# Small experts of a mixture-of-experts layer: chunks of 1024 channels, one gather and one scatter for all four

## The chip, the cores and the metric

The kernel runs on one core of a Trainium2 chip. The metric is the device time of one launch in microseconds (us), lower is better. Before the change the median of three runs is 2088.52 us (2086.04 to 2092.03).

## What is computed

Two blocks in a row on 256 tokens of 1024 channels, in float32. The second layer of the first block ends in a mixture of eight experts (`moe_swiglu`), and the second block first works on a context of 256 tokens of its own, which depends on nothing of the first block. Cut to what matters here:

```python
logits = xf @ w_router; top_vals, top_idx = top_k(logits, 2); gates = softmax(top_vals)
# each token goes to two of 8 experts, D_MODEL = 1024, D_FF_EXPERT = 3584
y = (silu(xb @ w1[e]) * (xb @ w3[e])) @ w2[e]          # xb: tokens of expert e
out = segment_sum(y * gate, token)                     # added back to 256 tokens
```

## The kernel before

The experts are put in order of how many tokens they have, and get room for 256, 128, 128, 128, 32, 32, 32, 32 tokens (`CAPS`). The last four are the small experts. Each has 42 MB of weights (w1, w3, w2 of 1024 x 3584 floats), as much as the biggest has, for 32 tokens. All weights of the kernel come as raw tiles of 1 MB (128 partitions x 2048 floats) over SP's queue. A big product splits a raw tile on ScalarE and VectorE into a high and a low part (`whi`, `wlo`) and takes three fp32r products; the small experts take the raw tile (`sraw`) as it is, in plain f32, which the program turns into two TensorE instructions per product.

A small expert's 32 tokens are the stationary operand and fill 32 of the array's 128 columns. So four products, for four different quarters of the channels, stand side by side in four column groups (`tile_position=(0, 32 * j)`) and write 32 partitions each of one PSUM bank. `smalls` is a generator of steps: `up` multiplies a chunk of 512 channels by w1 (column groups 0 and 1, 256 channels each) and w3 (groups 2 and 3), tile by tile, with half of a raw tile from each matrix and so two transfers of 512 KB; then Tanh and two VectorE operations make the gated product `eg` (64 partitions). `down` of the chunk before transposes `eg` (`ptg`, L1312), copies it on ScalarE to `gT` and multiplies it at once by two tiles of w2 (`sy`); the sums stay in `yacc`. Every small expert gathers its own tokens (`gather_x`: products `pg` of the hidden rows with a 0/1 matrix `oh`, and `gather_T`: `pgT`, `pgs`) and scatters its result (`scatter`: four masked copies `og` and eight products `pz<-yacc`).

The steps are dealt out between the units of big products. `drive` runs units of n raw tiles and holds up to `nhl` tiles' parts ahead; after each unit `balance` runs n x `rate` small steps. There are two such stages. In the first (`Mc`, the context stage here) the big units are the second block's context layers, `WITH_CTX` = 3 steps to a unit. In the second (`Mx`, the first expert's stage) they are `expert256(0)`, `WITH_EXPERT` = 2. Small steps that are left run alone afterwards (`for _ in smalls: pass`, the tail here), and then `experts128` takes the three middle experts (`h`, `y`). A small tile goes through a ring of four buffers (`sraw="b"`), in which a load can only be issued when TensorE has finished with the tile four places earlier; SP issues loads strictly in the order of the program. `fence` keeps the next big product on TensorE behind the last product of the small step. Beside units and small steps there are side generators (attention, mLSTM, gates), whose steps `tick` deals out once per unit. Product names: `gT`, `gk`, `go` context products, `hps` and `acc` the first expert's up and down products.

Of the kernel before, what the change touches and what calls it, by code (L numbers as in the profile page):

```python
# [36 lines left out]
WITH_CTX, WITH_EXPERT, ATTEND, MLSTM = 3, 2, (2.5, 3), 4  # L37
# [6 lines left out]
def _shape_consts():  # L44
# [6 lines left out]
    c["iota2"] = np.broadcast_to(np.arange(P) % 32, (P, P))  # L51
# [7 lines left out]
    c["quarter"] = (p // 32 == f[:, :4])  # L59
# [30 lines left out]
    moe = ("before", "iota", "iota2", "lt8", "eid", "caps", "quarter")  # L90
    names, packs = {}, []
    for part in (("ident",), early, late, moe):
# [80 lines left out]
class Kern:  # L173
    def __init__(self, ctx, tc, A, out):
# [9 lines left out]
        self.fence, self.in_small = None, False  # L184
# [32 lines left out]
    def drive(self, units):  # L217
        it, queue, held, nxt = iter(units), deque(), 0, None
        while True:
# [20 lines left out]
            if n:  # L240
                if self.later:
                    self.later.popleft()()
                self.tick()
# [12 lines left out]
    def tick(self):  # L256
        for s in list(self.sides):
            s.acc += s.rate
# [18 lines left out]
    def balance(self, big, small, rate):  # L277

        acc = 0.0
        for n in big:  # L280
            acc += n * rate
            while acc >= 1:
                self.in_small = True
                end = next(small, self) is self
                self.in_small = False
                if end:
                    break
                acc -= 1

# [56 lines left out]
    def mm(self, out, lhsT, rhs, start, stop, **kw):  # L346
        i = self.nc.tensor.matmul(out, lhsT, rhs, start=start, stop=stop, **kw)  # L347
# [47 lines left out]
    def gemm_out(self, loads, X, first, evict):  # L395
# [19 lines left out]
        def rest(w):  # L415
            first()
            for t in range(2):
                for n in range(2):
                    part(w[n], 0, n, t, False)
                    with self.lift():  # L420
                        evict(t, n, pts[t, n])
        for n in range(2):
            yield 1, prep(4, n), lambda w, n=n: half(w, n)
        yield 2, lambda: [prep(0, n)() for n in range(2)], rest
# [112 lines left out]
    def to_T_(self, z, X, tag, full):  # L537
        nc = self.nc
        for t in range(2):
            ts = slice(t * P, (t + 1) * P)  # L540
            for j in range(2):
                pt = self.bank(tag, "ptT")
                for kk in range(4):
                    k = 4 * j + kk
                    nc.tensor.transpose(pt[:, kk * P:(kk + 1) * P], z[:, t, k * P:(k + 1) * P], self.ident)
# [87 lines left out]
    def mixer(self, i, X, h, z1, e, S, ada):  # L633
# [58 lines left out]
        def p_T():  # L692
            pt = self.bank("a", "ptp")
            for k in range(2):
                for t in range(2):
                    nc.tensor.transpose(pt[:, k * 256 + t * P:k * 256 + (t + 1) * P], S.pin[:, t, k * P:(k + 1) * P], self.ident)
# [107 lines left out]
    def attn_side(self, i, S):  # L804
# [27 lines left out]
        for jp in range(2):  # L832
# [5 lines left out]
            for hh in range(2):  # L838
                pt = self.bank("c", "ptP")
                for h4 in range(4):  # L840
                    nc.tensor.transpose(pt[:, h4 * P:(h4 + 1) * P], s[:, hh * 4 + h4], self.ident)
# [183 lines left out]
    def moe(self):  # L1025
# [5 lines left out]
        with self.psum("M", a=4, s=2, b=2):  # L1031
# [4 lines left out]
            with (self.phase("Mc", 2, rows=1, wraw="xx", sraw="b"),  # L1036
                  tc.tile_pool(name="ctx", bufs=1) as self.hp):
                self.second_setup()
# [9 lines left out]
                self.balance(self.rest(), smalls, 1)  # L1048
# [32 lines left out]
    def first_rest(self, X):  # L1081
# [3 lines left out]
        def begin():  # L1085
# [5 lines left out]
            self.side(self.router(full, self.hp.tile([P, D], F32, name="route", tag="hs")), 3, 2000)  # L1091
# [22 lines left out]
    def gather_x(self, p, s0, cap):  # L1114

        nc, mp = self.nc, (self.smp if cap == 32 else self.mp)
        wide = max(cap, P)
        oh = mp.tile([P, 2, wide], F32, name="oh", bufs=2 if cap == 128 else 1)
        iota = self.C("iota2") if cap == 32 else self.C("iota")[:, s0:s0 + cap]
        for t in range(2):  # L1120
            nc.vector.tensor_scalar(oh[:, t], iota, self.place[:, t, p:p + 1], None, op0=ALU.is_equal)
        if cap == 32:
            x = mp.tile([P, 8, 32], F32, name="xs", bufs=2)
        else:
            x = [mp.tile([P, 8, cap], F32R, name=n, bufs=1 if cap == 256 else 2) for n in ("xeh", "xel")]
        per = min(8, 512 // cap)
        for j in range(8 // per):
            pt = self.bank("s" if cap == 32 else "a", "pg")
# [6 lines left out]
            if cap == 32:  # L1135
                nc.scalar.activation(x[:, sl], v, AF.Copy)
            else:
                self.split(x[0][:, sl], x[1][:, sl], v)
        return x, oh

    def gather_T(self, p, cap, oh):

        nc, mp = self.nc, (self.smp if cap == 32 else self.mp)
        nt = max(cap, P) // P
        ohT = mp.tile([P, nt, T], F32R if cap == 128 else F32, name="ohT", bufs=2 if cap == 128 else 1)
        gs = mp.tile([P, 2], F32, name="gs", bufs=4)
        pt = self.bank("s" if cap == 32 else "a", "pgT")
        for s in range(nt):
            for t in range(2):
                nc.tensor.transpose(pt[:, s * 256 + t * P:s * 256 + (t + 1) * P], oh[:, t, s * P:(s + 1) * P], self.ident)  # L1150
# [1034 lines left out]
```

## Time and profile before

| | before |
|---|---|
| median of 3 runs | 2088.52 us |
| profiled execution: its time, its span | 2086.75 us, 2085.0 us |
| TensorE busy, share of the span | 1957.8 us, 94% |
| VectorE, ScalarE busy | 66%, 49% |
| mean granted TensorE clock | 0.973 |
| DMA over the span | 541 MB, 260 GB/s |

Busy is the union of the instructions' spans on an engine, idle the rest. A row that gives a releaser says what ended the idle time just before an instruction. "PEclk" is the granted TensorE clock as a share of 2.4 GHz. Times are from the span's start. The small experts run from about 558 to 1296 us: the context stage from 558 to 893, the first expert's stage from 893 to 1253, the tail from 1253 to 1296.

### The profile page before, as it was taken

How to read it: one execution, taken by the hardware profiler on the slowest of the kernel's cores; microseconds unless marked ns; L12 is line 12 of the kernel's file. 1: busy time of each engine (PE TensorE's matmuls, PEld its weight loads, DVE VectorE, ACT ScalarE, POOL GpSimd, SP SyncE). 2: the span in 40 equal slices, each digit the busy share in tenths (PEclk: the TensorE clock that was granted, in tenths of full speed). 3: DMA queues.
4: the chain of work that ended last, by engine and by line, in shares of the span. 5: the costliest groups of instructions: out<-in, count | busy, mean ns of one | idle time of the engine just before them, and what ended most of it. 6: DMA issues, size and time to landing. Idle time of an engine off the chain costs nothing. (4 is left out here: it accounts for less than half of the span.)

```text
span 2085.0 us, 34522 instructions
## 1 busy us (share of the span) xinstructions
PE 1957.8 (94%) x13388; PEld 1557.5 (75%) x13388; DVE 1382.2 (66%) x2567; ACT 1013.3 (49%) x1696; POOL 85.3 (4%) x164
## 2 busy tenths in 40 slices
PE   6999999899998999899999997999999988998997
PEld 6768889687766676588878864787887858877876
DVE  8767445786657356645443433888888888887977
ACT  4534434344435333443333321767767745865774
POOL 1000000101000001000000000000000012011100
PEclk9999999899899999999999999999999999999999
DMA  8558785654797788998999999999999864334330
GB/s 288 171 195 298 243 287 195 218 165 135 258 325 263 261 283 302 323 349 326 385 383 377 335 343 356 388 355 331 346 341 335 320 209 129 100 110 122 102 101 31
DMA packets 302668, 541.13 MB, mean 260 GB/s; under 512 B 12688, under 2 KB 126112, under 8 KB 302240
## 3 DMA queue, kind: packets, MB, share of 16 engines
q1 hardware_dynamic: 301104, 534.73, 74.0%
q0 software_dynamic: 1104, 3.79, 0.6%
q8 instruction: 107, 1.75, 0.4%
q14 instruction: 65, 0.53, 0.1%
q10 hardware_dynamic: 288, 0.33, 0.0%
HBM read 533.33 MB, written 1.05 MB: 256 GB/s over the span
## 5 line engine op out<-in xcount | busy, mean ns | idle before, releaser
L335 DVE TENSOR_TENSOR wlo<-wraw,whi 128x1024 fp32r<-128x1024 f32 x572 | 677.7, 1226 | 178.8 <-ACT whi L334 175.3
L334 ACT ACTIVATE whi<-wraw 128x1024 fp32r<-128x1024 f32 x572 | 569.9, 1051 | 182.3 <-PE gT L347 44.1
L347 PE MATMUL gT<-xhi,whi 128*128 128x256 f32 x720 | 216.2, 302 | 17.1 <-ACT up L1641 9.7
L347 PE MATMUL gT<-xlo,whi 128*128 128x256 f32 x720 | 209.8, 292 | 1.4 <-DVE xlo L428 0.9
L347 PE MATMUL gT<-xhi,wlo 128*128 128x256 f32 x720 | 209.1, 293 | 0.0
L347 PEld LDWEIGHTS gT<-xhi,whi 128*128 128x128 f32 x720 | 142.5, 198 | 33.2 <-ACT up L1641 11.2
L347 PEld LDWEIGHTS gT<-xlo,whi 128*128 128x128 f32 x720 | 142.6, 198 | 3.2 <-DVE xlo L428 1.4
L347 PE MATMUL su<-sraw,xs 128*32 128x256 f32 x1792 | 138.1, 390 | 7.3 <-DMA sraw<-in_moe_w 6.6
L347 PEld LDWEIGHTS gT<-xhi,wlo 128*128 128x128 f32 x720 | 141.9, 198 | 3.0 <-issue 2.7
L347 PE MATMUL h<-wlo,xeh 128*128 128x512 f32 x336 | 133.1, 396 | 2.2 <-DVE wlo L335 2.2
L347 PE MATMUL h<-whi,xeh 128*128 128x512 f32 x336 | 132.2, 393 | 2.0 <-DVE z L1161 2.0
L347 PE MATMUL h<-whi,xel 128*128 128x512 f32 x336 | 131.4, 391 | 0.0
L347 PE MATMUL hps<-xeh,whi 128*128 128x256 f32 x448 | 128.4, 287 | 0.0
L347 PE MATMUL hps<-xel,whi 128*128 128x256 f32 x448 | 126.8, 283 | 0.0
L347 PE MATMUL hps<-xeh,wlo 128*128 128x256 f32 x448 | 126.6, 283 | 0.0
L893 DVE TENSOR_TENSOR gg<-gg,hps 128x256 f32<-128x256 f32 x50 | 20.9, 419 | 131.0 <-ACT gg L892 131.0
L347 PEld LDWEIGHTS su<-sraw,xs 128*32 128x32 f32 x1792 | 58.5, 111 | 59.1 <-DMA sraw<-in_moe_w 12.2
L347 PE MATMUL gk<-whi,xhi 128*128 128x512 f32 x240 | 99.6, 415 | 1.2 <-ACT whi L334 1.2
L347 PE MATMUL hps<-xhi,whi 128*128 128x256 f32 x352 | 100.2, 285 | 0.0
L347 PE MATMUL hps<-xlo,whi 128*128 128x256 f32 x352 | 99.6, 283 | 0.0
L347 PE MATMUL hps<-xhi,wlo 128*128 128x256 f32 x352 | 99.5, 283 | 0.0
L892 ACT ACTIVATE gg<-hps 128x256 f32<-128x256 f32 x50 | 19.0, 381 | 165.3 <-PE hps L347 163.5
(467 smaller groups left out, 4159.1 us busy)
## 6 DMA issues: line engine op xcount, KB each, us to landing
wraw<-in_moe_w SPq DMA_DIRECT2D x168, 1024.0 KB, 7.6
sraw<-in_moe_w SPq DMA_DIRECT2D x224, 512.0 KB, 8.4
wraw<-in_w_in SPq DMA_DIRECT2D x58, 1024.0 KB, 7.3
sraw<-in_moe_w SPq DMA_DIRECT2D x56, 1024.0 KB, 8.9
wraw<-in_ffn_w SPq DMA_DIRECT2D x33, 1024.0 KB, 5.5
wraw<-in_w_ada SPq DMA_DIRECT2D x24, 1024.0 KB, 5.4
wraw<-in_w_out SPq DMA_DIRECT2D x14, 1024.0 KB, 5.6
wraw<-in_w_in SPq DMA_DIRECT2D x24, 512.0 KB, 6.4
```

The source lines that it names most:

```text
L334: nc.scalar.activation(hi[:, a:b], raw[:, a:b], AF.Copy)
L335: i = nc.vector.tensor_sub(lo[:, a:b], raw[:, a:b], hi[:, a:b])
L347: i = self.nc.tensor.matmul(out, lhsT, rhs, start=start, stop=stop, **kw)
L892: nc.scalar.activation(g, pt[:, :256], AF.Silu)
L893: nc.vector.tensor_mul(g, g, pt[:, 256:])
```

## The change

A chunk is 1024 channels (the last of an expert 512). A raw tile holds one matrix only, so that a load is one transfer of 1 MB; w1 and w3 both use all four column groups, each group a quarter of the chunk, and w1's and w3's sums lie in the two halves of the PSUM bank. The last chunk's products are 128 columns wide instead of 256, so that there are twice as many of them. `eg` fills 128 partitions; its transposes (`turn`) stand at the end of the following chunk's `up`, one step ahead of the `down` that uses them. The four experts' 128 places are gathered by one set of `pg` products, with gates put into the matrix for the way back, and scattered by four products at the very end. A small step now takes two raw tiles, and the rates become 2 and 0.92. Side steps are dealt out in parts before and between the small steps. The fence binds transposes too. The last unit of the context layer's output product is cut in two (`by_n`). Two tables of constants are gone and four load into the router's own buffer; the row of `head_g` for the context is loaded later, when it is needed.

Steps: before, a chunk took 6 steps of one tile; now a chunk of 1024 takes 6 steps of two tiles. Of the 168 small raw tiles, TensorE's order had 75 ahead of the first `hps` product, 70 up to the last one and 23 after it; now it has 106, 62 and 0.

```diff
-WITH_CTX, WITH_EXPERT, ATTEND, MLSTM = 3, 2, (2.5, 3), 4
+WITH_CTX, WITH_EXPERT, ATTEND, MLSTM = 2, 0.92, (2.5, 3), 4
...
-    def balance(self, big, small, rate):
-        acc = 0.0
+    def balance(self, big, small, rate, between=True):
+        acc, self.between = 0.0, between
         for n in big:
             acc += n * rate
+            part = 1 / (1 + int(acc))
+            if between:
+                self.tick(part)
             while acc >= 1:
                 self.in_small = True
                 end = next(small, self) is self
                 self.in_small = False
+                if between:
+                    self.tick(part)
...
+    def turn_(self, out, x, ident):
+        return self.behind(self.nc.tensor.transpose(out, x, ident))
...
+        if by_n:
+            for n in range(2):
+                yield 1, prep(0, n), lambda w, n=n: rest_n(w, n)
+            return
         yield 2, lambda: [prep(0, n)() for n in range(2)], rest
...
+        chunks = [(c0, min(1024, FE - c0)) for c0 in range(0, FE, 1024)]
+        x = mp.tile([P, 8, P], F32, name="xs")
+        ohT = mp.tile([P, T], F32, name="ohTs")
+        y = mp.tile([P, D], F32, name="ys")
+
+        def gather():
+            oh, og = (mp.tile([P, 2, P], F32, name=n, tag="eg", bufs=2) for n in ("ohs", "ohg"))
+            for t in range(2):
+                for i, p in enumerate(ps):
+                    place, it = self.place[:, t, p:p + 1], self.C("iota")[:, :32]
+                    nc.vector.tensor_scalar(oh[:, t, group(i)], it, place, None, op0=ALU.is_equal)
+                    nc.vector.tensor_scalar(og[:, t, group(i)], it, place, self.gate[:, t, p:p + 1], op0=ALU.is_equal, op1=ALU.mult)
+            for j in range(2):
+                pt = self.bank("s", "pg")
+                for kk in range(4):
+                    k = j * 4 + kk
+                    for t in range(2):
+                        self.mm(pt[:, kk * P:(kk + 1) * P], self.h[:, t, k * P:(k + 1) * P], oh[:, t], t == 0, t == 1)
+                nc.scalar.activation(x[:, j * 4:j * 4 + 4], pt.rearrange("p (k s) -> p k s", s=P), AF.Copy)
+            pt = self.bank("s", "pgT")
+            for t in range(2):
+                self.turn_(pt[:, t * P:(t + 1) * P], og[:, t], self.ident)
+            nc.scalar.activation(ohT, pt[:, :T], AF.Copy)
+
+        def up(i, S, c0, n, prev):
+            part, kn = n // 4, 2048 // n
+            pt = self.bank("s", "su")[:, :2 * part]
+            for k0 in range(0, 8, kn):
                 for m, name in enumerate(("moe_w1", "moe_w3")):
+                    w = self.wraw(self.w_up(name, ps[i], c0, n, k0, kn), kn, n, "sraw")
+                    for kk in range(kn):
+                        for j in range(4):
+                            mm = self.mm(pt[group(j), m * part:(m + 1) * part], x[:, k0 + kk, group(i)],
+                                         w[:, kk, j * part:(j + 1) * part], not (k0 or kk or m), m == 1 and k0 + kk == 7,
+                                         tile_position=(0, 32 * j))
...
+                    self.fence = last = mm
+                if k0 + kn < 8:
+                    yield
+            if prev:
+                turn(*prev)
+            g = S.g = mp.tile([P, 256], F32, name="eg", bufs=2)[:, :part]
+            nc.scalar.activation(g, pt[:, :part], AF.Tanh, scale=0.5)
...
+            yield
+
+        def turn(i, S, c0, n):
+            part = n // 4
+            pg = self.bank("s", "ptg")
+            for b in range(0, part, P):
+                self.turn_(pg[:, b:b + P], S.g[:, b:b + P], self.ident)
...
+        def down(i, S, c0, n):
...
+            for f in range(0, nb, 2):
+                w = self.wraw(self.w_down(ps[i], c0 // P + f, 2), 2, 1024, "sraw")
...
+                if f % 4 and f + 2 < nb:
                     yield
+            for q in range(4):
+                out = y[group(i), q * 256:(q + 1) * 256]
...
+        def scatter():
+            for t in range(2):
+                for n in range(2):
                     pz = self.bank("s", "pz")
+                    self.mm(pz, ohT[:, t * P:(t + 1) * P], y[:, n * 512:(n + 1) * 512], True, True)
                     self.add_z(t, n, pz)
                 yield
```

TensorE at the end of the first expert before: `sy` and `su` are small products (128x.. or 32x256 is the moving operand's shape), `ptg` the transposes of `eg`, `pz<-yacc` a small expert's scatter, `h` the first products of the middle experts. A row of the order counts a plain f32 product once, for which the trace has two instructions.

```order
L1150 MATMUL pgT<-const_88,oh 128x128 x2
L347 MATMUL pgs<-gates,oh 128x1 x2
L347 MATMUL sy<-sraw,gT 32x256 x16
L347 MATMUL su<-sraw,xs 32x256 x2
L1312 MATMUL ptg<-const_88,eg 128x64 x2
L347 MATMUL su<-sraw,xs 32x256 x30
L347 MATMUL sy<-sraw,gT 32x256 x8
L1312 MATMUL ptg<-const_88,eg 128x64 x2
L347 MATMUL sy<-sraw,gT 32x256 x24
L347 MATMUL pz<-yacc,og 128x256 x5
L347 MATMUL h<-whi,xeh 128x512
L347 MATMUL pz<-yacc,og 128x256 x3
```

And now, at the same place (`pz<-yg` is the first expert's own scatter, `pg`, `pgT` and `pgs` the gather of the first middle expert):

```order
L353 MATMUL pz<-yg_8673,ohT 128x512
L353 MATMUL pz<-yg_8672,ohT 128x512
L353 MATMUL pz<-yg_8673,ohT 128x512
L353 MATMUL pg<-oh,z_64 128x128 x16
L356 MATMUL pgT<-const_88,oh 128x128 x2
L353 MATMUL pgs<-gates,oh 128x1 x2
L353 MATMUL h<-whi,xeh 128x512
L353 MATMUL h<-wlo,xeh 128x512
L353 MATMUL h<-whi,xel 128x512
```

No small product stands after the first expert any more; the gather of the middle expert, which lay among small products, stands alone between the scatter and `h`.

SP's queue in the middle of the context stage before (`sraw` small tiles, two rows of 128x2x512 to a tile, `wraw` a big unit's tile; ISA rows set an address):

```order
L320 DMA sraw<-in_moe_w 128x2x1024
L1294 ISA
L1294 DMA sraw<-in_moe_w 128x2x512
L1294 ISA
L1294 DMA sraw<-in_moe_w 128x2x512
L1294 ISA
L1294 DMA sraw<-in_moe_w 128x2x512
L1294 ISA
L1294 DMA sraw<-in_moe_w 128x2x512
L1501 DMA wraw<-in_w_in 128x8x128 x2
L1294 ISA
```

And now:

```order
L1540 DMA wraw<-in_w_in 128x8x128 x2
L326 ISA
L326 DMA sraw<-in_moe_w 128x2x1024
L326 ISA
L326 DMA sraw<-in_moe_w 128x2x1024
L326 ISA
L326 DMA sraw<-in_moe_w 128x2x1024
L326 ISA
L326 DMA sraw<-in_moe_w 128x2x1024
L326 DMA wraw<-in_w_in 128x4x512
```

Where three small tiles stood between two big ones on average, there are four, each one row of 1 MB.

## Rows read from the trace of the kernel before

**Rows 1.** Part 1 of the page: busy microseconds, share, instructions of each engine.

```profile
PE 1957.8 (94%) x13388; PEld 1557.5 (75%) x13388; DVE 1382.2 (66%) x2567; ACT 1013.3 (49%) x1696; POOL 85.3 (4%) x164
```

**Rows 2.** By stage: start and end, length, busy of each engine, PEclk, DMA share, GB/s.

```profile
558.00:893.00 335.00, 307.54 (x2443) 212.42 (x2443) 194.72 (x495) 125.09 (x278) 12.69 (x38) 0.95 0.85 295
893.00:1253.00 360.00, 354.47 (x3113) 287.01 (x3112) 150.92 (x207) 120.19 (x182) 0.00 (x0) 1.00 0.98 356
1253.00:1296.00 43.00, 31.61 (x297) 16.23 (x296) 8.88 (x23) 7.31 (x13) 0.00 (x0) 0.88 0.95 357
1296.00:1680.00 384.00, 377.86 (x1699) 303.26 (x1699) 328.89 (x318) 267.99 (x303) 0.00 (x0) 1.00 0.95 345
```

**Rows 3.** TensorE groups by shape: count, then busy, mean ns, idle before and its releasers.

```profile
L347 PE MATMUL su<-sraw,xs 128*32 128x256 f32 x1792 | 138.1, 390 | 7.3 <-DMA sraw<-in_moe_w 6.6 <-ACT xs L1136 0.5
L347 PE MATMUL sy<-sraw,gT 128*32 128x256 f32 x896 | 65.2, 393 | 14.0 <-DMA sraw<-in_moe_w 9.8 <-ACT gT L1314 4.2
L347 PE MATMUL pg<-oh,z 128*128 128x32 f32 x128 | 16.1, 283 | 0.3 <-DVE oh L1121 0.3
L347 PE MATMUL pz<-yacc,og 128*128 128x256 f32 x64 | 18.9, 426 | 1.1 <-ACT yacc L1331 1.1
L1312 PE MATMUL ptg<-const,eg 64*128 64x64 f32 x56 | 9.4, 247 | 2.2 <-DVE yacc L1325 0.6 <-DVE gs L1156 0.5 <-ACT xs L1136 0.5
L347 PE MATMUL pgs<-gates,oh 128*128 128x1 f32 x36 | 4.8, 240 | 0.5 <-ACT ohT L1151 0.5
L1150 PE MATMUL pgT<-const,oh 128*128 128x128 f32 x18 | 3.4, 282 | 0.5 <-DVE yacc L1328 0.5
L347 PE MATMUL pg<-oh,z 128*128 128x128 f32 x96 | 13.6, 280 | 0.0
L347 PE MATMUL pg<-oh,z 128*128 128x256 f32 x32 | 8.9, 446 | 0.0
L347 PE MATMUL pz<-yg,ohT 128*128 128x512 f32 x16 | 7.1, 599 | 0.0
L1219 PE MATMUL ptg<-const,es 128*128 128x128 f32 x84 | 12.6, 273 | 0.0
```

**Rows 4.** Waits of TensorE in 1253 to 1296: total, times, longest.

```profile
PE sy L347 <- DMA sraw<-in_moe_w: 6.5, 5, 1.6
PE su L347 <- DMA sraw<-in_moe_w: 3.8, 8, 0.7
```

**Rows 5.** Timeline of TensorE: start, length, instruction, count, idle before and releaser.

```profile
1099.81 3.66 PE L347 MATMUL su<-sraw,xs 128*32 128x256 f32 x64
1113.38 1.93 PE L347 MATMUL sy<-sraw,gT 128*32 128x256 f32 x32 [0.38 <-ACT gT L1314]
...
1271.71 0.63 PE L347 MATMUL su<-sraw,xs 128*32 128x256 f32 x4 [0.30 <-DMA sraw<-in_moe_w]
1274.43 0.63 PE L347 MATMUL su<-sraw,xs 128*32 128x256 f32 x4 [0.31 <-DMA sraw<-in_moe_w]
...
1283.58 1.07 PE L347 MATMUL sy<-sraw,gT 128*32 128x256 f32 x16 [1.12 <-DMA sraw<-in_moe_w]
1286.23 1.93 PE L347 MATMUL sy<-sraw,gT 128*32 128x256 f32 x16 [1.57 <-DMA sraw<-in_moe_w]
1288.74 1.94 PE L347 MATMUL sy<-sraw,gT 128*32 128x256 f32 x16 [0.58 <-DMA sraw<-in_moe_w]
```

**Rows 6.** Waits of SP's DMA queue in 558 to 1297, the two longest of sraw loads.

```profile
SPq L1294 <- PE sy L347: 121.2, 31, 8.9
SPq L320 <- PE su L347: 117.6, 32, 15.6
```

**Rows 7.** Stretches of the context stage, columns as in rows 2.

```profile
558.00:620.00 62.00, 57.23 (x507) 38.68 (x510) 30.17 (x68) 19.65 (x44) 2.21 (x5) 0.94 0.89 312
800.00:893.00 93.00, 80.41 (x671) 55.63 (x672) 54.95 (x133) 34.99 (x64) 3.74 (x9) 0.95 0.93 333
```

**Rows 8.** Tile oh on VectorE: minimum, median, maximum ns, first and last start.

```profile
L1121 DVE TENSOR_SCALAR oh<-const,places x16: 275/278/353, 553.6 to 1266.5; 128x128 f32<-128x128 f32 x14, 128x256 f32<-128x256 f32 x2
```

More of the change, by code (lines that the diff above doesn't have):

```diff
@@ L89, in _shape_consts @@
     early, late = ("amask", "diag"), ("perm", "cos", "sin")
-    moe = ("before", "iota", "iota2", "lt8", "eid", "caps", "quarter")
+    moe, route = ("iota",), ("before", "lt8", "eid", "caps")
     names, packs = {}, []
-    for part in (("ident",), early, late, moe):
+    for part in (("ident",), early, late, moe, route):
         off, cols = 0, []
@@ L242, in drive @@
                     self.later.popleft()()
-                self.tick()
+                if not self.between:
+                    self.tick()
                 yield n
@@ L288, in balance @@
                 acc -= 1
+        self.between = False
     def lift(self):
@@ L1090, in begin @@
             self.to_T(self.h, X, "a", full)
-            self.side(self.router(full, self.hp.tile([P, D], F32, name="route", tag="hs")), 3, 2000)
+            self.side(self.router(full, self.route), 3, 2000)
         yield act(begin)
@@ new lines, in up @@
+        def up(i, S, c0, n, prev):
+            part, kn = n // 4, 2048 // n
+            pt = self.bank("s", "su")[:, :2 * part]
+            for k0 in range(0, 8, kn):
+                for m, name in enumerate(("moe_w1", "moe_w3")):
+                    w = self.wraw(self.w_up(name, ps[i], c0, n, k0, kn), kn, n, "sraw")
[4 more added lines that the diff above has]
+                                         tile_position=(0, 32 * j))
+                            if not kk and not j and (k0 or m):
+                                self.tc.add_manual_dep(mm.ins, last.ins.name, AFTER, reason="the bank's first products open both halves")
+                    self.fence = last = mm
[5 more added lines that the diff above has]
+            nc.scalar.activation(g, pt[:, :part], AF.Tanh, scale=0.5)
+            nc.vector.scalar_tensor_tensor(g, g, 1.0, pt[:, :part], op0=ALU.add, op1=ALU.mult)
+            nc.vector.scalar_tensor_tensor(g, g, 0.5, pt[:, part:], op0=ALU.mult, op1=ALU.mult)
+            yield
@@ L1330, in scatter @@
[L1330 to L1338 removed]
+            for q in range(4):
+                out = y[group(i), q * 256:(q + 1) * 256]
+                if c0:
+                    nc.vector.tensor_add(out, out, ys[group(q)])
+                else:
+                    nc.vector.tensor_copy(out, ys[group(q)])
@@ L1349, in smalls @@
-        prev, S = None, begin(ps[0])
-        for i, c in [(i, c) for i in range(len(ps)) for c in range(nchunk)] + [(None, None)]:
-            if c is not None:
-                if c == 0 and i:
-                    S = ready
-                yield from up(ps[i], S, c)
-                if c == 2:
-                    S.ohT, S.gs = self.gather_T(ps[i], 32, S.oh)
-                if c == nchunk - 1 and i + 1 < len(ps):
-                    ready = begin(ps[i + 1])
+        gather()
+        prev = None
@@ L1359, in smalls @@
+        for i, c in [(i, c) for i in range(len(ps)) for c in chunks]:
+            S = SimpleNamespace()
+            yield from up(i, S, *c, prev)
             if prev:
                 yield from down(*prev)
-                if prev[2] == nchunk - 1:
-                    yield from scatter(prev[1])
-            prev = c is not None and (ps[i], S, c)
+            prev = (i, S, *c)
+        turn(*prev)
+        yield from down(*prev)
+        yield from scatter()
     def second_setup(self):
@@ L1540, in start @@
             H.vt = self.vals[l, s] = c2([P, 2, P], "vt")
-            if full:
+            if full and not s:
                 H.hgr = self.row(A["head_g_2"][l], 512, nc.gpsimd)
@@ L1768, in ev_out @@
                 done(t)
-        yield from self.gemm_out(load, mix, finish_m, ev_out)
+        yield from self.gemm_out(load, mix, finish_m, ev_out, s)
     def values(self, H, ps, late=True):
```

142 lines of the change are left out of this document (51 added, 91 removed).

## Prediction

> **What bounds the kernel now.** I read the busy times first: TensorE is busy 1957.8 of 2085 us [rows 1], so an edit counts by the TensorE time it takes away, or by the idle time it closes. Next the busy times by stage [rows 2], since the edit lives in 558 to 1296 us. The reader is to see three stages. In the context stage (335 us) TensorE is busy 307.5, granted clock 0.95, DMA share 0.85 at 295 GB/s. In the first expert's stage (360 us) it is busy 354.5 at clock 1.00, DMA share 0.98 at 356 GB/s: both are full. In the tail (43 us) it is busy 31.6 at clock 0.88, DMA share 0.95. The stage behind, 1296 to 1680, has 377.9 of 384 busy; nothing there is edited and I leave it as it is. Then the groups by shape [rows 3] for prices, the waits and the timeline of the tail [rows 4, 5] for who is late there: small products wait for their raw tile, 6.5 + 3.8 = 10.3 us in 13 waits. Last the waits of SP's queue [rows 6]: its loads wait 121.2 and 117.6 us, in the two longest groups, for TensorE to give a small tile back. So the ring of four is what couples loads to products.
>
> The sum is made against the profiled execution, 2086.75 us (span 2085.0); that is 1.8 below the median of the runs, and I add 1.8 at the end.
>
> **The change part by part.**
>
> *Products of the small experts.* One raw tile is 8 products, 16 instructions; 64 of them took 3.66 us [rows 5], 0.915 a tile. 168 tiles stay 168 tiles, and the columns stay the same. In the last chunk of each expert 128 instructions of 128 columns stand for 64 of 256. No row has a 128-column product in a column group. Lower bound: nothing, since on the full array halving the columns halves the time (gather, 13.6 / 96 = 0.142 us against 8.9 / 32 = 0.278 [rows 3]); upper bound: each costs what the wide one does, 4 x 3.66 = +14.6. Below nothing is excluded, as no column goes away. I take the row on the full array: 0.
>
> *Gather.* Four gathers of 32 columns took 16.1 us in 128 instructions; now there are 32 of 128 columns, 32 x 0.142 = 4.5. Gain 11.6. Of `pgs` 16 of 36 instructions go: 4.8 x 16/36 = 2.1. Of `pgT` 8 of 18 become 2: 3.4 x 6/18 = 1.1 [rows 3].
>
> *Scatter.* `pz<-yacc` took 18.9 us. Four products of 512 columns are 8 instructions like those of the first expert's scatter, 7.1 / 16 = 0.444 each, 3.6 together [rows 3]. Gain 15.3.
>
> *Transposes.* 56 of `eg` took 9.4 us. Now each expert has 7 of 128x128, 28 in all, at the middle experts' 12.6 / 84 = 0.15: 4.2. Gain 5.2. Since `turn` stands a step ahead of `down`, the 4.2 us in which `sy` waited for the copy `gT` go, and the 1.1 before `pz<-yacc` [rows 3]. Gain 5.3. What is late next there is `sy` waiting for its raw tile, which is counted below.
>
> *The tail.* 23 tiles stood there alone, and the order now has none. Their products are not saved; they are done earlier. What goes is the waiting, 10.3 us [rows 4], and the half clock it brought: two blocks of 16 `sy` took 1.93 where a block at full clock took 1.07 [rows 5], 1.7 together. Gain 12.0. The gather of the first middle expert, which lay among those products, now stands bare before `h`. The copies between its products and the first `h` had small products over them; without cover I take 1.5 us (bounds 0 and 4.5, its whole 32 x 0.142 once more).
>
> *The start.* The joint gather needs 16 small VectorE operations where two stood. `oh` took 0.278 us in its median [rows 8], so at most 14 x 0.278 = 3.9 more, at least 0 if the loads of the first tiles are later than that anyway. I take 1.5.
>
> *Where the tiles go.* The context stage gets 106 tiles instead of 75, the first expert's stage 62 instead of 70. Moving costs TensorE nothing in sum, but the context stage may become bound by loads. Its TensorE time: 335 + 31 x 0.915 = 363.4, less what is saved inside it (one gather 4.0, one scatter 4.7, two `pgT` and `pgs` 1.8, 13 of 28 turns 1.8): 351.1. Its loads: 335 us x 295 GB/s = 98.8 MB, and 31 x 1.049 MB = 32.5 more, 131.3 MB. At the 356 GB/s of the first expert's stage [rows 2] that is 368.8 us. So both limits lie within 5%. I take the middle, 360: 9 us above the TensorE sum. Bounds: 0, if loads keep up, and 70, at 312 GB/s (131.3 MB in 421), the rate of 558 to 620 [rows 7]. Small loads are now one transfer of 1 MB with rows of 4 KB. In the tail, where nothing but loads sets the pace, tiles of that kind (`sy`) came every (1288.74 - 1283.58) / 2 = 2.58 us, those of two 512 KB transfers (`su`) after 2.72 [rows 5], 407 against 386 GB/s. That is why I don't take the upper end.
>
> The Trainium skill, "DMA: Bandwidth & Descriptors", section "Bandwidth", advises transfers of 1 MiB or more and measured 341 GB/s for one such transfer and 425 for 16 MB. The two tile periods above agree in direction; by its 425 the context stage's loads would take an estimated 309 us and TensorE alone would bound it, the sum being 9 us lower.
>
> *Edits at nothing.* VectorE and ScalarE are busy 195 and 125 of 335 us in the context stage [rows 2], so four narrow additions in the place of one and the wider Tanh are hidden there; if not, the PSUM bank of `sy` comes back late, which the bank after next feels. The constants' load, the later load of `head_g` and the cut output unit change no TensorE work; the load has the first half of the output product in front of it. SP issues 28 x 4 = 112 loads for `up` where it issued 224.
>
> *Sum:* 11.6 + 2.1 + 1.1 + 15.3 + 5.2 + 5.3 + 12.0 = 52.6 gained; 9 + 1.5 + 1.5 = 12.0 lost; 40.6 net. 2086.75 - 40.6 = 2046.2, plus 1.8: 2048.
>
> **The rivals.**
>
> *The context stage loses its waits.* For: side steps now stand between small steps, so a side chain on VectorE or ScalarE has two tiles, 1.8 us, of small products over it, and the stage has 27.5 us of idle TensorE [rows 2] to win. Against: its DMA share was already 0.85. If loads cost no 9 us and half the idle time goes (13.8), 2048 - 9 - 13.8 = 2025.
>
> *The clock falls in the context stage.* The tail shows it: with a wait of some 0.3 to 1.6 us before each tile the granted clock was 0.88 and blocks ran at half of it [rows 2, 5]. The context stage, with few such waits, had 0.95. If 31 more tiles bring it to 0.88, its TensorE work, 307.5 + 28.4 - 12.3 = 323.6, takes 323.6 x 0.95 / 0.88 = 349.3, 26 more: 2074. The Trainium skill says the same in "TensorE: Matmul & The Clock Gate", section "HAM oscillation — how this bites in real kernels": waits for loads between short bursts of products bring the clock back to its lower level. The tail agrees. Against it in the context stage: big products stand between the small ones, so idle stretches are cut short.
>
> *The ring sets the pace, slower than before.* Place: SP's queue in the context stage. Four tiles are now taken between two big units where three were, and the ring holds four. A load can be issued only when TensorE gives a tile back, and the big unit's own load stands behind four of them in the same queue, so a late ring also delays the split of big weights and then everything behind on TensorE. If the stage does not get above 312 GB/s [rows 7], it takes 421 us instead of 360: 2048 + 61 = 2109. It decides from 400 us on, that is below 328 GB/s; there the whole gain is gone. For it: SP's waits [rows 6], and the stage's mean of 295. Against: from 800 to 893 the same ring made 333 [rows 7], in the next stage 356 with a second ring beside it, and where the rate was low TensorE was the slower side.
>
> *The change doesn't do what it says.* The order has one gather, four products in the scatter and no tile in the tail, so this can't be; only the half-wide products can cost their upper bound, 2063, which lies in the forecast's own range.
>
> **How the numbers follow.** Forecast 0.56, with a range of its own of 2034 to 2066 (9 us of loads less, the 14.6 of narrow products more, and a few us of either sign). Waits lost 0.15 (2025). Clock 0.13 (2074). Ring 0.16, spread around its break-even: 0.09 above, 0.07 within. This kernel can't be told from no change within 0.3%, 6 us. Faster takes the forecast, the lost waits and nearly all of the clock case: 0.83. Same: 0.07 of the ring and 0.01 of the clock, 0.08. Slower: 0.09. For 8 times in 10 the range must reach into the cases at both ends: 2028 cuts off half of the lost waits (0.07), 2086 leaves out about 0.12 of the ring and a little of the clock.
>
> **What would show it.** Right, if the changed profile has `pg` of small experts near 4.5 us, `pz` of them near 3.6, the transposes near 4.2, no waits for `gT`, the first `h` right behind the first expert's scatter and gather, near 1256 us, and a context stage (first `su` to first `hps`) of about 360 us at 360 GB/s. The step on half-wide products is wrong if 128 of them take clearly more than 3.66 us. The forecast is wrong on the low side if the context stage stays near 340 with less idle time, on the high side if it passes 375: then rows of `su` waiting for `sraw` say loads, and a granted clock of 0.9 or less with equal waits says clock. It fails altogether if that stage is above 400.

## The result and the profile after

The changed kernel takes 2065.05 us (median of 4 runs, 2063.87 to 2070.27) against 2087.28 (4 runs, 2085.17 to 2092.03) beside it: ratio 0.9895, 95% interval 0.9871 to 0.992. It is faster, the way that was forecast, by about 22 us; 40.6 were forecast. Ratios go by the fast runs alone; one execution of `sides_old` below, 4672.79 us, is left out of its ratio for that. 2065 lies in the range (2028 to 2086) and at the upper edge of the likeliest case's own (2034 to 2066).

The profiled execution of after took 2065.54 us, its span is 2063.5: 21.5 below before's 2085.0. First the page's busy times, which answer to [rows 1]:

```profile
PE 1923.4 (93%) x13442; PEld 1530.3 (74%) x13442; DVE 1372.2 (66%) x2555; ACT 1011.7 (49%) x1663; POOL 84.2 (4%) x165
```

TensorE is busy 34.4 us less than in [rows 1] while the span fell by 21.5 only, so its idle time grew by 12.9. The forecast had 37.0 us of busy time going (its sum without the waits) and 3.6 us of idle time (15.6 of waits out, 12.0 in). So the busy side is right within 2.6 us, and the idle side is off by 16.5. (The 2.6 is partly luck; the account of the half-wide products below says why.)

Where the idle time came, the stages show. They are cut here by instructions, so that both kernels are cut alike: from the first `su` to the first `hps` (context stage), from there to the first `h` (the first expert's stage, in before with its tail), and the next 366 to 373 us up to a later `h` (middle experts). Columns as in [rows 2]. Before:

```profile
558.80:899.40 340.60, 313.61 (x2475) 217.94 (x2475) 200.21 (x502) 130.34 (x284) 12.69 (x38) 0.95 0.85 296
899.40:1295.80 396.40, 379.48 (x3373) 297.31 (x3374) 154.12 (x224) 121.67 (x188) 0.00 (x0) 0.99 0.98 355
1295.80:1668.80 373.00, 367.26 (x1654) 295.19 (x1653) 320.83 (x309) 263.48 (x297) 0.00 (x0) 1.00 0.95 345
```

After:

```profile
561.20:959.40 398.20, 341.10 (x3037) 222.86 (x3037) 201.41 (x506) 129.89 (x277) 12.09 (x39) 0.91 0.93 334
959.40:1282.70 323.30, 320.21 (x2874) 265.24 (x2874) 148.47 (x199) 116.04 (x162) 0.00 (x0) 1.00 0.97 358
1282.70:1648.70 366.00, 362.55 (x1647) 294.83 (x1647) 314.81 (x303) 267.34 (x296) 0.00 (x0) 1.00 0.92 333
```

The reader is to see two large numbers of opposite sign. The context stage grew by 57.6 us, the first expert's stage with the tail shrank by 73.1. The start is 2.4 later, the middle experts are 7.0 shorter, the end 1.4: 2.4 + 57.6 - 73.1 - 7.0 - 1.4 = -21.5. The forecast had the context stage 25 us longer (335 to 360). Its 335 is a window of [rows 2] and ends some 6 us ahead of the first `hps`, where before has 340.6 us; so growth is to be compared with growth: 57.6 came, 25 were forecast, 32.6 too few. In this stage TensorE's idle time went from 27.0 to 57.1 us, the granted clock from 0.95 to 0.91, and the DMA share from 0.85 to 0.93, no further.

The groups by shape of after, which answer to [rows 3]:

```profile
L353 PE MATMUL su<-sraw,xs 128*32 128x256 f32 x1536 | 112.1, 408 | 13.6 <-DMA sraw<-in_moe_w 13.1 <-ACT xs L1326 0.5
L353 PE MATMUL sy<-sraw,gT 128*32 128x256 f32 x896 | 61.3, 399 | 5.3 <-DMA sraw<-in_moe_w 5.3
L353 PE MATMUL su<-sraw,xs 128*32 128x128 f32 x512 | 16.4, 275 | 0.5 <-DMA sraw<-in_moe_w 0.5
L356 PE MATMUL ptg<-const,eg 128*128 128x128 f32 x28 | 6.7, 305 | 3.0 <-DVE ys L1380 3.0
L353 PE MATMUL pg<-ohs,z 128*128 128x128 f32 x32 | 4.1, 281 | 2.6 <-DVE ohs L1318 2.6
L353 PE MATMUL pz<-ys,ohTs 128*128 128x512 f32 x8 | 3.8, 592 | 0.0
L353 PE MATMUL pgs<-gates,oh 128*128 128x1 f32 x20 | 2.5, 234 | 0.0
L356 PE MATMUL pgT<-const,oh 128*128 128x128 f32 x10 | 1.7, 272 | 0.0
L356 PE MATMUL pgT<-const,ohg 128*128 128x128 f32 x2 | 0.4, 272 | 0.0
```

Gather, scatter and transposes are down to 4.1, 3.8 and 6.7 us. `sy` no longer waits for `gT`. `su` now waits 13.1 + 0.5 = 13.6 us for its raw tile, where it waited 6.6, and `sy` 5.3, where it waited 9.8.

Last the timeline of after around the first `h`, where before had its tail [rows 5]:

```profile
1269.96 7.45 PE L353 MATMUL pz<-yg,ohT 128*128 128x512 f32 x16
1278.48 3.81 PE L353 MATMUL pg<-oh,z 128*128 128x128 f32 x32 [1.07 <-DVE oh L1147]
1282.13 0.38 PE L356 MATMUL pgT<-const,oh 128*128 128x128 f32 x2
1282.35 0.50 PE L353 MATMUL pgs<-gates,oh 128*128 128x1 f32 x4
1282.71 0.48 PE L353 MATMUL h<-whi,xeh 128*128 128x512 f32 x1
```

The tail is gone: scatter, gather and `h` follow each other with one wait of 1.07 us.

### The profile page after: what moved, and what is told of

Its sections match the earlier page's. It is cut to its first block, busy times and chain, and to the rows that moved or that the text cites. A ratio compares the mean times of both kernels' runs of the same rounds, so it can differ in the third digit from the quotient of the medians.

```text
span 2063.5 us, 34203 instructions
## 1 busy us (share of the span) xinstructions
PE 1923.4 (93%) x13442; PEld 1530.3 (74%) x13442; DVE 1372.2 (66%) x2555; ACT 1011.7 (49%) x1663; POOL 84.2 (4%) x165
## 5 line engine op out<-in xcount | busy, mean ns | idle before, releaser
L353 PE MATMUL su<-sraw,xs 128*32 128x256 f32 (+1 forms) x2048 | 128.5, 375 | 14.1 <-DMA sraw<-in_moe_w 13.6
L353 PE MATMUL gk<-wlo,xhi 128*128 128x512 f32 x240 | 99.3, 414 | 2.5 <-DVE wlo L341 2.3
```

The costliest lines, as they stand in the source:

```text
L353: return self.behind(self.nc.tensor.matmul(out, lhsT, rhs, start=start, stop=stop, **kw))
```

## The experiments

All start from the changed kernel, except `old_moved`, which starts from the kernel before. "Context stage" and "first expert's stage" are cut as above; their lengths in the changed kernel are 398.2 and 323.3 us.

### Is it the loads or TensorE that holds the context stage?

`half_loads`: the `w3` products read the tile of `w1`, and the tiles of `w3` are never loaded.

```
-  w = self.wraw(self.w_up(name, ps[i], c0, n, k0, kn), kn, n, "sraw")
+  if not m:
+      w = self.wraw(self.w_up(name, ps[i], c0, n, k0, kn), kn, n, "sraw")
```

> w3's products of the small experts read w1's tile, and w3's tiles are not loaded: 28 of an expert's 42 tiles are multiplied as before, 14 fewer are loaded; the output is not the reference's. Theory L (the context stage is bound by the transfers: 398 us at a DMA share of 0.93, its waits and its clock of 0.91 follow from that): some 37 of 106 tiles fewer, 2.6 us each, 96 us of transfers go, TensorE's own work is the bound again: context stage 345 to 362 us at a clock of 0.95 or more, whole 2000 to 2030. Theory C (the clock falls because small and big products alternate, whatever the loads do): context stage 385 or more at 0.91, whole 2045 or more. Theory S (the new dealing of the side steps and the kept order delay the big units): 380 to 398.

`half_products`: all tiles are loaded, half of the `up` products are made (the mark of the sum's last product moves with them).

```
-  for kk in range(kn):
+  for kk in range(kn // 2):
 ...
```

> Half of the products of the small experts' up part are left out (the second half of each raw tile is not multiplied), all loads stay; the output is not the reference's. It takes 74 x 0.46 = 34 us of TensorE work out of the context stage and no byte. Theory L (bound by transfers): the context stage stays within 13 us of 398. Theory C (TensorE at a low clock is the bound): it falls by 34 / 0.91 = 37 or more, to about 360. Theory S: falls by about 34 too, since the delays of side chains stay.

The context stages, first of `half_loads`, then of `half_products`:

```profile
562.80:886.10 323.30, 311.57 (x3035) 217.30 (x3035) 198.28 (x508) 128.75 (x276) 12.05 (x39) 0.99 0.83 293
```

```profile
566.40:957.20 390.80, 315.79 (x2380) 209.30 (x2380) 201.92 (x506) 129.43 (x276) 12.24 (x39) 0.87 0.93 338
```

With the same products and fewer loads the stage takes 323.3 us, 74.9 less, and TensorE is nearly full at clock 0.99; the whole took 1986.54 us (one run). With the same loads and fewer products it takes 390.8, 7.4 less, with the same DMA share and a clock of 0.87; the whole took 2058.99 (one run). So loads hold the stage. The low clock is a consequence: it rises when the loads go, and falling to 0.87 it lengthened nothing. `half_loads` came out below what its own theory of loads gave (345 to 362 for the stage, 2000 to 2030 for the whole): the same products need 323.3 us at most, not some 350. It leaves one thing open: a load that is gone takes its transfer with it and its wait for a free tile too, and this run doesn't separate the two.

### The order of the side steps

`sides_old`: side steps only between big steps, as before.

```
-  self.balance(big, smalls, WITH_CTX)
+  self.balance(big, smalls, WITH_CTX, False)
```

> The side steps of the context stage are dealt out as before the change (all after a big unit), everything else is the changed kernel. Theory S (the new dealing costs): context stage at least 10 us shorter than 398, whole 2055 or less. Theory L: the transfers set the pace, within 8 us of 398 either way, whole 2057 to 2075.

Ratio to the kernel before 0.9896 (0.9866 to 0.9926), against 0.9895 of the changed kernel; its context stage took 400.4 us. How side steps are dealt out is worth nothing that these runs can tell.

### The tiles moved alone

`old_moved`: the kernel before with 22 tiles moved from its tail into the earlier stages by the two rates; chunks, transfers, gathers stay.

```
-WITH_CTX, WITH_EXPERT, ATTEND, MLSTM = 3, 2, (2.5, 3), 4
+WITH_CTX, WITH_EXPERT, ATTEND, MLSTM = 4, 1.75, (2.5, 3), 4
```

> The kernel before with its rates alone changed to 4 and 1.75, so that its tiles lie 97, 63 and 8 in the context stage, the first expert's stage and the tail, where they lay 75, 70, 23. Old chunks, gathers, scatters. Theory L: 22 more tiles, 2.7 us of transfers each, on the 289 us of transfers that the stage had (340.5 us at 0.85), at a share of 0.93: context stage about 375; what leaves the tail and the first expert's stage is about 20 us of products and 8 of waits: whole 2087 + 35 - 28, 2088 to 2100. Theory C or S: the stage grows by the 20 us of products alone, 360, whole 2072 to 2082.

2116.34 us, ratio 1.0142 (1.0107 to 1.0177): slower than I had expected. Its context stage, and the one behind it:

```profile
560.40:980.70 420.30, 369.90 (x2889) 241.12 (x2889) 209.79 (x523) 134.42 (x294) 11.68 (x38) 0.91 0.84 293
980.70:1329.80 349.10, 343.44 (x2966) 277.63 (x2966) 152.36 (x209) 120.18 (x179) 0.00 (x0) 1.00 0.99 360
```

With the old chunks the context stage takes in the tiles at the old 293 GB/s: it grows by 79.7 us, and the rest shrinks by 47.3. Moving tiles off the tail alone is a loss. Something in the rest of the change makes it a gain. It isn't the transfers alone: this stage has its transfers busy for 0.84 of the time only, where the changed kernel has 0.93.

### The form of the transfers

`half_rows` loads each tile of `up` in two transfers by column halves (rows of 2 KB, as before the change); `half_k` in two by halves of k (rows of 4 KB).

```
 # half_rows; both take the place of w = self.wraw(...)
+for hh in range(2):
+    ...dma_start(w[:, :, hh * n // 2:(hh + 1) * n // 2], self.w_up(name, ps[i], c0 + hh * n // 2, n // 2, k0, kn))
 # half_k
+for hh in range(2):
+    ...dma_start(w[:, hh * kh:(hh + 1) * kh], self.w_up(name, ps[i], c0, n, k0 + hh * kh, kh))
```

> The changed kernel with each small tile of w1 and w3 loaded by two transfers of 512 KB with rows of 2 KB (1 KB in an expert's last chunk), as before the change, into the same tile; products, order and ring are the same. Theory T (the new transfers, one of 1 MB with rows of 4 KB, are what lets the context stage hold 106 tiles): 74 of the 106 tiles take 2.72 instead of 2.58 us at the least, context stage 398 + 10 to 430, whole 2072 or more. Rival O (old transfers are as fast; the stage of the old kernel with its tiles moved was slow for the old order and chunks): within 4 us of 398, whole 2060 to 2070.

> The changed kernel with each small tile of w1 and w3 loaded by two transfers of 512 KB, split by input channels, so that the rows keep 4 KB (2 KB in the last chunk). Theory row (the length of the rows made the loads faster): as the changed kernel, 2060 to 2070. Theory count (the number of transfers did): as with two transfers of 2 KB rows, 2079 to 2089.

`half_rows`: 2085.27 us, ratio 0.9992 (0.9978 to 1.0006). The whole gain is gone. `half_k`: 2072.34, ratio 0.9932 (0.991 to 0.9955), between what its two theories gave. Of the 20 us between 2065 and 2085 some 13 lie between the two ways of halving a load, and 7 between one load and two with the same rows; the 7 aren't clear of noise, as the intervals of `half_k` and the changed kernel touch. The first two stages of `half_rows`:

```profile
565.90:971.90 406.00, 353.62 (x3036) 222.77 (x3036) 201.62 (x506) 129.83 (x276) 12.17 (x39) 0.95 0.94 325
971.90:1300.10 328.20, 323.48 (x2874) 266.63 (x2873) 148.69 (x199) 116.95 (x163) 0.00 (x0) 1.00 0.99 354
```

The DMA share is as high as in the changed kernel or higher, 0.94 and 0.99, while fewer bytes come through, 325 and 354 GB/s against 334 and 358. The transfers themselves are slower: 406.0 x 0.94 = 382 us in the context stage against 398.2 x 0.93 = 370. The two stages are 7.8 and 4.9 us longer. Most of the rest of the 17.5 us between the two spans lies ahead of the first `su` (4.7), where `r175`, with whole loads, is as late.

But the expectation that products and order stay the same didn't hold. TensorE takes a tile's 16 instructions in two pieces now, 4 and 12, with other products between them:

```profile
624.95 0.62 PE L353 MATMUL su<-sraw,xs 128*32 128x256 f32 x4
...
627.09 1.06 PE L353 MATMUL su<-sraw,xs 128*32 128x256 f32 x12
```

```profile
L353 PE MATMUL su<-sraw,xs 128*32 128x256 f32 x1536 | 130.9, 389 | 9.2 <-DMA sraw<-in_moe_w 8.6 <-ACT xs L1326 0.5
```

Together they take 1.68 us where 16 in one piece took 1.07, and the group is busy 130.9 us instead of 112.1. In `half_k` the pieces are 8 and 8, 0.64 us each, and the group takes 114.2. So the 13 us between `half_rows` and `half_k` have two possible causes, the shorter rows and the smaller pieces, and no run separates them.

### Fewer tiles in the context stage

`r175` and `r150` move tiles back to the first expert's stage.

```
-WITH_CTX, WITH_EXPERT, ATTEND, MLSTM = 2, 0.92, (2.5, 3), 4
+WITH_CTX, WITH_EXPERT, ATTEND, MLSTM = 1.75, 1.1, (2.5, 3), 4
+WITH_CTX, WITH_EXPERT, ATTEND, MLSTM = 1.5, 1.25, (2.5, 3), 4
```

> The changed kernel with rates of 1.75 and 1.1: 92 tiles in the context stage and 76 in the first expert's stage, instead of 106 and 62. Theory L (bound by the transfers): the context stage's transfers take 289 + 17 x 2.58 = 333 us, at a share of 0.93 358 us; the first expert's stage takes 14 tiles more, 36 us of transfers, and is bound by them at 350 to 356: whole about 7 us below the changed kernel, 2052 to 2062. If the stage were bound by TensorE or its clock: context stage 398 - 13 = 385, first expert's stage 336, whole 2065.

> Rates of 1.5 and 1.25: 80 and 88 tiles. Theory L: context stage near TensorE's own 340 us (transfers 302), first expert's stage bound by 26 tiles more of transfers, about 380 to 388 us: whole 2065 to 2078, no better than the changed kernel. So the gain by rates ends between 106 and 80 tiles.

Both missed: 2082.31 us (ratio 0.9986, 0.9967 to 1.0005) and 2086.44 (1.0003, 0.9986 to 1.002). Their two stages, first `r175`, then `r150`:

```profile
566.70:937.30 370.60, 322.38 (x2808) 217.68 (x2809) 201.39 (x500) 128.44 (x274) 12.22 (x39) 0.92 0.89 319
937.30:1302.30 365.00, 343.48 (x3103) 275.18 (x3102) 151.47 (x205) 117.59 (x165) 0.00 (x0) 0.97 0.96 356
```

```profile
565.90:895.90 330.00, 300.76 (x2615) 207.97 (x2616) 195.75 (x490) 126.37 (x272) 12.04 (x39) 0.95 0.89 318
895.90:1303.10 407.20, 363.08 (x3296) 281.83 (x3295) 156.02 (x215) 118.60 (x167) 0.00 (x0) 0.95 0.94 351
```

The context stage shrinks by 27.6 and 68.2 us, and the first expert's stage, where loads are at 351 to 358 GB/s in each run, grows by 41.7 and 83.9. The second stage was full (DMA share 0.97, TensorE 320.2 of 323.3 us), and what is given back to it costs more than it saves. It costs more than the transfers of 14 and 26 tiles, too (36 and 67 us at 2.58): in `r150` the share is down to 0.94 and the clock to 0.95, so waits came in, and why wasn't tried. The change's split is the better one although its context stage is the longest of the three.

### More buffers

`ring5x` takes one of the context layers' two big tiles as a fifth small one; `uring` lets big and small tiles go round one ring of all six.

```
 # ring5x
-phase("Mc", 2, rows=1, wraw="xx", sraw="b")
+phase("Mc", 2, rows=1, wraw="x", sraw="bbbby")
 # uring
-self.rings["wraw"] = "xx"
+self.rings["wraw"] = self.rings["sraw"] = "bbxbbx"   # with one counter
```

> The changed kernel with a fifth small tile in the context stage, taken from the big units, which have one raw tile instead of two there. Theory ring (the transfers stand still for 7% of the stage, 28 of 398 us, because a load waits for a tile to come back): DMA share rises towards 0.97, context stage 375 to 388, whole 2045 to 2058. Theory engines (370 us of transfers and the uneven work of TensorE are the floor): 393 or more, and more if the single big tile makes the split late, whole 2062 to 2085.

> The changed kernel with one ring of six raw tiles for small and big loads together in the context units, instead of four and two. Theory ring: a small load waits for the tile six places earlier, context stage 378 to 390, whole 2048 to 2060. Theory engines: within 6 us of 398, whole 2060 to 2072; more if a big tile that waits for its split holds up the small loads behind it.

> The version with one ring of six raw tiles again, in more rounds: as before, 2056 to 2062 if its gain on the changed kernel (6 us, 0.3%) is real, 2063 to 2067 if it was chance.

`ring5x`: 2068.09, ratio 0.9895 (0.9862 to 0.9929), context stage 397.1: no gain, but it takes a buffer from the big tiles, so it doesn't show what a fifth one by itself is worth. `uring`: 2058.66, 0.9857 (0.9832 to 0.9882), and again 2060.9, 0.9871 (0.9847 to 0.9896); context stage 392.5 and 390.7. It has the lowest medians, 4 to 6 us below the changed kernel's, but the intervals overlap with 0.9871 to 0.992. What got shorter in its context stage is TensorE's wait for small tiles: 7.7 + 1.7 = 9.4 us in `uring`, 12.9 + 4.2 = 17.1 in the changed kernel.

### The big tiles' rows

`big_rows`: the context layers' big tiles are read as 128 rows of 8 KB.

```
-src = w2d[k0 * P:(k0 + kn) * P, c0:c0 + n].rearrange("(k p) n -> p k n", p=P)
+src = w2d[k0 * P:(k0 + 1) * P, c:c + 2048].rearrange("p (k n) -> p k n", n=n)
 ...
```

> The changed kernel, but the big units' weight tiles of the context layers are read as 128 rows of 8 KB from other places of the same matrices (the same number of bytes and transfers of 1 MB; the output is not the reference's). They have rows of 512 bytes to 2 KB. Theory rows: 106 small tiles take 106 x 2.58 = 273 of the stage's 370 us of transfers, so the 20-odd big tiles take some 97, 4 to 5 us each, because of their short rows; with long rows about 45 us of transfers go, and the stage comes to TensorE's own 351 to 365 us, whole 2018 to 2035. Theory bytes: the length of the big tiles' rows matters little, the stage stays at 388 to 400, whole 2055 to 2067.

2064.45 us, ratio 0.9883 (0.9851 to 0.9915). Its context stage:

```profile
562.30:957.40 395.10, 338.17 (x3036) 221.99 (x3037) 203.42 (x506) 129.78 (x277) 12.63 (x39) 0.93 0.89 336
```

The DMA share fell to 0.89, so that the transfers take 395.1 x 0.89 = 352 us instead of 370; the stage fell by 3.1 only. Cheaper transfers of the big tiles leave it as long. So the sum of all transfers doesn't set its length by itself: `half_loads` took small tiles away and won 74.9 us, this run took some 18 us of transfers from the big ones and won next to nothing.

## Why the prediction was right, and where it was off

**Gather, scatter, small columns: right.** `pg` 16.1 to 4.1 (12.0; forecast 11.6), `pz` 18.9 to 3.8 (15.1; 15.3), `pgs` 2.3 (2.1), `pgT` 3.4 to 1.7 + 0.4, with the new `ohg` form (1.3; 1.1). The wait for `gT` is gone.

**Half-wide products at nothing: right.** The timeline of after has both widths at their shorter time:

```profile
838.17 1.07 PE L353 MATMUL su<-sraw,xs 128*32 128x256 f32 x16
...
849.58 1.06 PE L353 MATMUL su<-sraw,xs 128*32 128x128 f32 x32
853.67 0.44 PE L356 MATMUL ptg<-const,eg 128*128 128x128 f32 x2 [3.03 <-DVE ys L1380]
```

32 narrow take 1.06 us, 16 wide with the same columns 1.07. What the prediction missed here is a gain: `su` and `sy` together were busy 138.1 + 65.2 = 203.3 us and are 112.1 + 16.4 + 61.3 = 189.8, 13.5 less, of which 1.7 stood in the sum, for the tail. `half_rows`, in which `su` takes 22 us more, suggests that whole tiles help here, as their products aren't taken in pieces. With the groups above, 46.9 us of busy time went, and the rest of TensorE's work took 12.5 more: two misses that nearly cancel, and so the agreement within 2.6 us is partly luck.

**Transposes: 2.7 of 5.2.** They took 6.7 us where 4.2 were forecast. The price of 0.15 us each came from the middle experts; here two stand by themselves and take 0.44 us (last line above), or 0.38 like the pair of `pgT` at 1282.13. And the edit that I had at nothing shows once, with the sign that I had named for it: 3.0 us `ptg <-DVE ys L1380`, the narrow additions that give a bank back late. In `r175` that wait is 11.7 in sum, so it is a matter of where it falls.

**The tail: right.** It is gone with its waits. The bare gather behind it cost 1.07 (1.5), but not for the reason given: the wait is ahead of `pg`, for `oh` on VectorE, and `h` doesn't wait for the copies. The joint gather waits 2.6 us for `ohs` (1.5); the later start, 2.4, is of that size, though in traces of other versions the first `su` comes up to 5.5 us later still.

**The context stage: right in kind, wrong in size, and this is the step that failed.** The prediction put it at "360: 9 us above the TensorE sum". It is 398.2, and by growth the term of 25 us measured 57.6. The prediction's own signs say so: the stage passed the 375 above which it called itself wrong on the high side, with `su` waiting for `sraw`, which it named as the sign of loads; its rate is 334 GB/s, not 360; and the first `h` comes at 1282.7, not near 1256. I had two limits, 351.1 for TensorE and 368.8 for loads, and took "the middle": a value below one of the two limits, on the ground that small tiles had come every 2.58 us in the tail. The TensorE limit was no limit: it was before's stage with its idle time and its clock of 0.95, and `half_loads` makes the same products in 323.3 us. The rate is real. In the best stretches of this stage the loads do run so, but not in the others. Equal stretches of it in after, in order:

```profile
561.20:589.60 28.40, 22.29 (x226) 12.91 (x227) 13.79 (x24) 8.47 (x16) 0.00 (x0) 0.94 1.04 393
589.60:618.00 28.40, 27.14 (x287) 20.53 (x285) 8.73 (x25) 4.90 (x15) 2.21 (x5) 1.00 0.79 292
...
816.80:845.20 28.40, 20.34 (x140) 11.45 (x140) 11.79 (x32) 7.67 (x23) 3.62 (x2) 0.82 0.81 255
845.20:873.60 28.40, 24.37 (x267) 17.94 (x270) 13.91 (x25) 8.71 (x12) 0.24 (x1) 0.94 1.04 397
```

Stretches with the transfers full (393, 397 GB/s) and TensorE waiting stand next to stretches with the transfers at 0.79 and 0.81 (292, 255). In the first and the last line the transfers are at their limit, in the second TensorE nearly is (27.1 of 28.4 us), and in the third neither (20.3 of 28.4). The size would have come out of rows that I had: in before 340.6 us x 0.85 = 289 us of transfers in this stage, and 31 tiles x 2.58 = 80 more: 369. After has 398.2 x 0.93 = 370. So the loads limit was right (133.0 MB by its row, 131.3 forecast); the stage then took 28 us more, in which the transfers stood idle by turns. So of the 38 us between 360 and 398 the choice of the middle accounts for 9, and for 28 that the prediction had no term for what the two limits cost each other.

**Why they idle: in part open.** The waits of SP's queue from 561 to 1283 in after answer to [rows 6] (total, times, longest). [rows 6] shows two groups of before; a third, nearly as long, is the last line here:

```profile
SPq L326 <- PE su L353: 211.0, 79, 12.2
SPq L326 <- PE sy L353: 96.9, 42, 7.2
SPq L326 <- DVE wlo L341: 62.0, 17, 7.9
```

```profile
SPq L1294 <- PE su L347: 105.6, 24, 13.0
```

So loads wait for TensorE to give small tiles back 121 times in after, 307.9 us in all, and 87 times, 344.4 us, in before. The sum of these waits is no longer than it was, so it doesn't tell the two kernels apart. TensorE's own waits in the context stage say more. Before:

```profile
PE su L347 <- DMA sraw<-in_moe_w: 2.8, 4, 1.5
PE sy L347 <- DMA sraw<-in_moe_w: 2.0, 1, 2.0
PE go L347 <- ACT whi L334: 0.6, 1, 0.6
PE go L347 <- DVE wlo L335: 0.5, 1, 0.5
```

After:

```profile
PE su L353 <- DMA sraw<-in_moe_w: 12.9, 11, 2.0
PE sy L353 <- DMA sraw<-in_moe_w: 4.2, 5, 1.4
PE ptA L356 <- ACT whi L340: 6.2, 1, 6.2
PE go L353 <- DVE wlo L341: 5.0, 1, 5.0
PE gT L353 <- DVE wlo L341: 2.7, 3, 1.2
PE gT L353 <- ACT whi L340: 2.5, 2, 1.3
PE go L353 <- ACT whi L340: 2.4, 1, 2.4
PE gk L353 <- DVE wlo L341: 1.5, 3, 1.0
```

TensorE's idle time here grew by 30.1 us. It waits 17.1 us for small tiles (4.8 before) and, in products of big weights, 14.1 for weights that are split late (1.1 before). Most of the rest is for other steps on VectorE and ScalarE, and the row of `ptA` belongs there in spite of its releaser: it transposes `prob` and reads no weight. So a part of the growth is the coupling by the ring that the third rival named. Not every late split is a late load, though. Ahead of the split that `go` waited 5.0 us for, VectorE had `hs<-hs,sz` to do, which waited for GpSimd:

```profile
829.39 1.29 DVE L2064 TENSOR_TENSOR hs<-hs,sz 128x512 f32<-128x512 f32 x2 [2.23 <-POOL sz L1774]
```

Six buffers in one ring took 6 to 8 us off the stage; a fifth small one in the place of a big one, the old side steps and longer big rows took off next to nothing. What keeps the other 20 us isn't shown by these runs: late splits are the next to look at, and no run aimed at them. A ring of six or eight small tiles beside both big ones was not run.

**The rivals.** "The ring sets the pace" came half way: 398.2 us lies between 360 and its 421, just under the 400 from which I had the whole gain gone. The gain isn't gone because the stages behind gave some 14 us more than forecast: the first expert's stage with the tail 73.1 (67), the middle experts 7.0 (0), the end 1.4 (0). That is luck: the prediction had no term for it, and without it the total would be near 2080, outside the likeliest case's own range. "The clock falls" happened in its sign (0.91), but `half_loads` and `half_products` show it as what the waits leave behind, not as the price. "The context stage loses its waits" fell: it got more.

**The transfer of 1 MB was worth more than I gave it.** In the prediction it was a reason not to take the upper end. `half_rows` shows it at the size of the whole net gain: without it the kernel stands at the time of before. That doesn't make the rest worth nothing. From `old_moved` to `half_rows`, where the loads keep their old form, it is 31 us (2116.34 to 2085.27), about what moving the tiles costs (2087 to 2116). The Trainium skill's larger figure ("DMA: Bandwidth & Descriptors", section "Bandwidth", 425 GB/s) is reached in none of the stretches shown; the fullest has 397.

**Not forecast:** the middle experts' 7.0 us. Before has 5.7 us of idle TensorE there and after 3.5, so most of the 7.0 is busy time. In `old_moved`, which has no long tail either, that stage is 366.0 too. So it seems to go with the tail; how was not tried.

## What to carry to other kernels

When work moves out of an exposed tail, ask how much transfer time (DMA share times length) the receiving stage has left, and price the moved loads in transfer time too; the larger of the two limits is the least that the stage can take, never the mean of both. Here 7% came on top (398 over 370 us). Take a TensorE limit from busy time at the clock that it can have, not from a stage's length with its waits in it. Halve the loads and halve the products in two runs before believing a clock or a wait: here only one of them moved the stage by much. Two loads of the same bytes are not the same load: compare row length and number of transfers first, and look whether TensorE takes the tile in one piece.

## What was not expected of the hardware

Loading tiles of `up` as one transfer with 4 KB rows instead of two with 2 KB rows was worth 20 us in 2085, at a lower DMA share (0.93 against 0.94, and 0.97 against 0.99); how much of it is the transfers and how much TensorE's smaller pieces stays open. Longer rows of the big tiles took some 18 us of transfers out of the context stage and shortened it by 3. Halving the products of a stage that loads bound lowered the granted clock from 0.91 to 0.87 and cost nothing, and halving its `up` loads raised it to 0.99.
